# Four expert blocks instead of two at the tile-by-tile end of layer 0, three modulation steps moved there, hyena transposes two projections later

## The chip, the cores and the metric

The kernel is one program on one core of a Trainium2 chip. The time is device microseconds of one execution. TensorE is called PE here (its weight loads PEld), VectorE DVE, ScalarE ACT, GpSimd POOL, and SyncE, whose queue issues most DMAs, SP.

## The reference

Two layers run over 256 latent and 256 context tokens of width 1024, all in float32. In layer 1 the context tokens only feed the latent ones, so only the latent half is carried on. Cut to what matters here:

```python
for l in range(DEPTH):                                   # 2 layers
    mod = (silu(c) @ w_ada[l] + b_ada[l])                # six rows of 1024: sh1 sc1 g1 sh2 sc2 g2; the same for c_ctx
    y, yc = mixer_sublayer(x * (1 + sc1) + sh1, ...)     # one projection to 2824 columns, four mixers, one back
    x = layer_norm(alpha * x + g1 * y)
    x = layer_norm(alpha * x + g2 * peer(x * (1 + sc2) + sh2))

def hyena(p, ...):
    p = dwconv(p, short_w) + short_b                     # three taps
    x0, x1, v = split(p, 3, -1)
    u = v * x1
    y = bidir_fftconv(u, k_fwd, k_bwd) + u * skip
    return y * x0

def peer(h, wq, sub_keys, u_tab, v_tab):                 # per token: 8 heads x 16 of 16384 single-neuron experts
    q = h @ wq; top 16 of 128 for each of two halves; top 16 of their sums; g = softmax
    act = gelu(h . u_tab[e]); return sum_e (g * act) * v_tab[e]
```

## The kernel before

**Planner.** The program is written in an order, and a planner then orders each engine's queue before the run: it simulates the engines, and a free engine takes the earliest-written instruction that is ready in that simulation; `low(3000)` puts an instruction far behind. On the chip each engine then works its queue strictly in that order. A tile pool with `bufs=n` is a ring: the next tile of a name waits until the tile n places before it has been read for the last time. `issue_after` holds an instruction behind a named one on the same queue.

**Split.** Most products are made of float32 numbers cut in two: ACT casts the high part (line 140), POOL or DVE subtracts for the low part (line 141), and `mm3` multiplies three times (lines 144 to 146).

**Projections** (`mixers`, line 372 on). 128 columns at a time, `projT` loads a weight tile (512 KB, `w_raw`, ring of 4 in layer 1), splits it, and multiplies it with hT, the modulated input. Eight split products of 512 tokens make one projection in layer 0 and for keys, values and scan inputs in layer 1; of 256 tokens for the others of layer 1. The order is: four for the convolution, six for hyena (loop over `i` in 4, 2, 5, 3, 0, 1), four for the scan (loop over 2, 0, 1, 3), the scan's time steps, two gates, and then keys, queries and values. The 31 taps of the convolution (line 368) are written as low-priority filling on DVE. Hyena's product `hv[4+m] = hv[4+m] * hv[2+m]` (line 389) has to be transposed on PE (line 404); the transposes of half m = 1 are written behind the first scan projection, those of m = 0 behind the second.

**Modulation steps** (`ada_steps`, line 253 on). Step c of layer l makes 512 of the 6144 columns: four transfers of 512 KB (`wa_raw`, line 261), sixteen products (`pm`, line 263), a copy on ACT (line 267), four small transposes (`pt`, line 281) and an addition on DVE (`modT`, line 282). The steps are one generator, worked off in order by whoever calls it. In layer 0's router one part is called behind each of the query projections, and behind the last of them `fill_to(1, (FL, 11)[l])` works off all that is left up to step FL of layer 1. The buffer ring for `wa_raw` is 3 there. Layer 1's first projections need steps 0 to 3 of layer 1, its output projection 4 and 5, its expert stage the rest.

**Router** (layer 0). Sixteen query projections, the top-16 searches, `pairs` on DVE; then the slots are transposed (`tr`, line 1208), turned into one-hot tiles (`o`, `Ah`, `Al`, `B_`, lines 1226 to 1242), multiplied into gate blocks (`G`, lines 1248 and 1249), and stored to DRAM (`Gd`). Up to 28 blocks of the first expert product, `u_stage` (`au`: activations of 128 experts for 384 tokens, 24 products each), are written between these. Two stand ahead of the slots' transposes, seven ahead of the gates.

**Expert loop** (line 1378 on). For each of 128 blocks of 128 experts: `weights(bl)` multiplies the activations with the gates and splits them (`wh`, `wl`, ring of 4), `values(bl)` loads 512 KB (`v_raw`, ring of 2) and splits them (`v_hi`, `v_lo`, ring of 2), and `accum` adds 36 products to six PSUM banks (`ov`): three tiles of 128 tokens, two halves of 512 columns. The fourth tile of layer 0 is gathered row by row instead (`gathered`), two rows per block. The last NE = 2 blocks are kept out of the loop: for them each half tile in turn gets its products of both blocks, so that tile 0 is complete first. Behind each tile come `combine` (gate, residual, statistics, norm) and `to_hT` (transposes `xT`, line 792, scale, split into hT), from which layer 1's projections start. The value split of block 127 has a pool of its own (`vep`); its `v_raw` is of the ring. `fill_to(1, FX)` with FX = 6 stands in the last tile and finds nothing to do, since FL is 6.

Of the kernel before, what the change touches and what calls it, by code (L numbers as in the profile page):

```python
# [41 lines left out]
XB = (96, 100, 104, 108)  # L42
VD = (10, 1)
UM = ((0, 2, 4, 6, 7), (0, 1, 2, 3, 4, 5, 6, 7))
NE = 2
WHB = (4, 5)
WB = 3
PW = (1, 1)
PU = (0, 1)
PRB = (4, 5)  # L50
FL = 6
FM = 11
LF = 200
NF = 2
# [32 lines left out]
def tile_hybrid_diffusion(ctx: ExitStack, tc: tile.TileContext, I: dict, out: bass.AP):  # L87
    nc = tc.nc
    V, S, G, T = nc.vector, nc.scalar, nc.gpsimd, nc.tensor
    uid = [0]  # L90

    def pool(name, bufs=1, stack=ctx, **k):
        uid[0] += 1
        if "space" not in k:
            k["reuse_waits"] = "tile"
        return stack.enter_context(tc.tile_pool(name=f"{name}{uid[0]}", bufs=bufs, **k))
# [222 lines left out]
    def mixers(l, mx, wp, hT, yT, dfts, side, side_s, more):  # L319
# [70 lines left out]
        for i in (2, 0, 1, 3):  # L390
            n = NT if i == 3 else 512
            b = projT(18 + i, n)
            xc = t2k([128, 512])
            short_conv(xc[:, :n], b, "scw", "scb", i, n)
            sig(xb[:, i, :n], xc[:, :n])
            V.tensor_tensor(xb[:, i, :n], xb[:, i, :n], xc[:, :n], ALU.mult)
            next(side, None)
            with low(3000):
                next(taps, None)
            if i in (2, 0):  # L400
                m = i // 2
                b = bank("ut")
                for t in range(NTL):
                    T.transpose(b[:, t * 128:(t + 1) * 128], hv[:, 4 + m, t * 128:(t + 1) * 128], ident)
                S.copy(un[:, :, :, m * 128:(m + 1) * 128].rearrange("p t s c -> p s t c"), b[:, :NT].rearrange("p (s t c) -> p s t c", t=2, c=128))
# [407 lines left out]
    prep = {}  # L813
# [33 lines left out]
    for l in range(2):  # L847
# [426 lines left out]
        with ExitStack() as vst:  # L1274
# [17 lines left out]
            def values(bl, p, n, eng=G):  # L1292
                raw = mk(vp, [128, D], tag="v_raw", bufs=VB[l])
                late["v", bl] = nc.sync.dma_start(raw, I["v"][l, bl])
                hi = mk(p, [128, D], F32R, tag="v_hi", bufs=n)
                lo = mk(p, [128, D], F32R, tag="v_lo", bufs=n)
                split(raw, hi, lo, eng)
                return hi, lo
# [75 lines left out]
                nc.gpsimd.dma_start(xd[t], x_)  # L1374

            gat = gathered() if GT else iter(())
            last = 128 - NE
            for st in range(UBl, last + UBl):
                if st < 128:
                    u_stage(st)  # L1380
# [11 lines left out]
            ws, vs_ = [], []  # L1392
            for bl in range(last, 128):
                ws.append(weights(bl))
                if bl < 127 or l:
                    vs_.append(values(bl, vp, VB[l], V))
            rg_s.close()
            xp_s = ExitStack()
            x_n = mk(pool("xp", stack=xp_s, side="right"), [128, len(DT), D], name="x_n")
            fle = ExitStack()  # L1400
            if l == 0:
                vs_.append(values(127, pool("vep", stack=fle, side="right"), 1, V))
            end = tc.issue_after(late["v", 127 - VD[l]].ins)
            end.__enter__()
            for i, t in enumerate(DT):
# [20 lines left out]
            end.__exit__(None, None, None)  # L1426
            if l == 0:
                prep.clear()
                prep.update(raw=(pool("fl", stack=fle, side="right"), 3))
            for i, t in enumerate(DT):  # L1430
                for hh in range(2):
                    with tc.issue_after(prev.ins):
                        for j in range(NE):
                            ins = accum(last + j, i, *ws[j], *vs_[j], (hh,))
                    prev = ins
                if i == len(DT) - 1 - FI and l == 0:
                    fill_to(1, FX)
                lst = mk(gp, [128, 1, 2, 6], tag="ln_st")
                r = x_n[:, i, :]
                combine(t, r, gb[t // 2], lambda hh: pacc[i, hh], lst, lnr if l else None)  # L1440
                if l == 0:
                    to_hT([t], lambda t: x_n[:, DT.index(t), :], lnc, hT, gp, hb=HB2)
# [119 lines left out]
```

## Time and profile before

| | |
|---|---|
| median of 3 runs (lowest to highest) | 2898.36 us (2893.72 to 2905.68) |
| the profiled execution | 2899.02 us, span 2897.2 us, mean granted clock 0.967 |
| PE busy | 2688.0 us (93% of the span) |
| DVE busy | 1996.6 us (69%) |
| ACT, POOL busy | 1098.8 us (38%), 595.0 us (21%) |
| DMA | 625.03 MB, mean 216 GB/s |

The busy time is a mean over stages, so it has to be read stage by stage. On the time axis of the profiled execution layer 0's router ends at 605 us, its gates and first expert products run to about 790 us, its expert loop to 1784 us, the layers meet between 1784 and 1810 us, and layer 1's projections follow until about 1922 us. A matmul is pipelined, so two successive ones overlap in the rows.

### The profile page before, as it was taken

The numbers are of one execution on the slowest core, as the hardware profiler recorded it, in microseconds if no ns is written. First come the engines' busy times: TensorE is split into PE (matmuls) and PEld (weight loads), VectorE is DVE, ScalarE is ACT, GpSimd is POOL, SyncE is SP. The second block draws the span as 40 slices with busy tenths as digits, with TensorE's granted clock in tenths as the row PEclk, the third lists the DMA queues.
The fourth block names the chain that finished last, engine by engine and source line by source line (L and its number), as shares of the span: only waits on it lengthen the run. The fifth ranks groups of instructions, "written<-read, shape, count | busy, mean of one in ns | idle before, by whom it ended". The sixth has DMA issues, their size and how long they took to land.

```text
span 2897.2 us, 41097 instructions
## 1 busy us (share of the span) xinstructions
PE 2688.0 (93%) x15342; PEld 2283.5 (79%) x15342; DVE 1996.6 (69%) x4247; ACT 1098.8 (38%) x1736; POOL 595.0 (21%) x439
## 2 busy tenths in 40 slices
PE   6797899889899999999999998889999999999997
PEld 3574566578899988888878886766889899999986
DVE  4956448969787777777777746974866655555556
ACT  2233532235433333333323334334334444444443
POOL 2233000033224444444334202430000000000000
PEclk9899999989999999999999998899999999999999
DMA  7222433347899998999889735325458976776656
GB/s 258 59 91 95 131 131 113 131 143 270 284 325 309 314 333 309 317 308 317 305 299 308 250 103 195 99 99 186 131 157 295 309 235 204 216 216 202 196 189 196
DMA packets 241836, 625.03 MB, mean 216 GB/s; under 512 B 22424, under 2 KB 104794, under 8 KB 236004
## 3 DMA queue, kind: packets, MB, share of 16 engines
q1 hardware_dynamic: 201156, 475.05, 50.4%
q0 software_dynamic: 40480, 147.36, 14.3%
q8 instruction: 120, 1.97, 0.3%
q14 instruction: 80, 0.66, 0.1%
HBM read 573.04 MB, written 49.30 MB: 215 GB/s over the span
## 4 chain that ended last, share of the span: by engine, by line
PE 39%; DMA 13%; issue 11%; DVE 9%; POOL 6%; ACT 1%; SPq 0%; POOLq 0%; DVEq 0%; ACTq 0%
DMA grow<-in_vg_dram,eu 9%; PE ov L144 5%; PE ov L145 5%; POOL grow L1344 5%; PE ov L146 5%; PE au L1017 4%; PE au L144 4%; PE au L146 4%; PE au L145 4%; DMA grow<-in_lnr_dram 2%; DVE accg L1357 1%; DVE yT L368 1%; PE G L1248 1%; PE G L1249 1%; DMA grow<-in_ug_dram,eu 1%
## 5 line engine op out<-in xcount | busy, mean ns | idle before, releaser
L146 PE MATMUL au<-hT,u_lo 128*128 128x384 f32 (+1 forms) x1744 | 552.6, 317 | 5.6 <-DVE u_lo L141 5.2
L144 PE MATMUL au<-hT,u_hi 128*128 128x384 f32 (+1 forms) x1744 | 553.4, 317 | 3.0 <-DVE slT L1212 3.0
L145 PE MATMUL au<-hT,u_hi 128*128 128x384 f32 (+1 forms) x1744 | 551.6, 316 | 0.0
L145 PE MATMUL ov<-v_lo,wh 128*128 128x512 f32 x1280 | 505.0, 395 | 27.7 <-DVE v_lo L141 27.7
L146 PE MATMUL ov<-v_hi,wl 128*128 128x512 f32 x1280 | 500.8, 391 | 0.0
L144 PE MATMUL ov<-v_hi,wh 128*128 128x512 f32 x1280 | 462.9, 394 | 12.1 <-ACT v_hi L140 6.5
L140 ACT CAST u_hi<-u_raw 128x1024 fp32r<-128x1024 f32 x218 | 228.9, 1050 | 447.0 <-PE au L145 303.7
L141 DVE TENSOR_TENSOR v_lo<-v_raw,v_hi 128x1024 fp32r<-128x1024 f32 x255 | 312.6, 1227 | 78.9 <-ACT v_hi L140 78.3
L141 DVE TENSOR_TENSOR u_lo<-u_raw,u_hi 128x1024 fp32r<-128x1024 f32 x194 | 237.1, 1222 | 165.5 <-ACT u_hi L140 165.5
L144 PEld LDWEIGHTS au<-hT,u_hi 128*128 128x128 f32 x1744 | 332.1, 190 | 11.0 <-DVE slT L1212 3.4
L146 PEld LDWEIGHTS au<-hT,u_lo 128*128 128x128 f32 x1744 | 331.6, 190 | 9.6 <-DVE u_lo L141 8.3
L145 PEld LDWEIGHTS au<-hT,u_hi 128*128 128x128 f32 x1744 | 331.9, 190 | 7.7
L140 ACT CAST v_hi<-v_raw 128x1024 fp32r<-128x1024 f32 x256 | 268.1, 1047 | 107.2 <-DMA v_raw<-in_v_dram 98.6
L145 PEld LDWEIGHTS ov<-v_lo,wh 128*128 128x128 f32 x1280 | 242.1, 189 | 82.4 <-DVE v_lo L141 38.3
L140 ACT CAST wh<-act 128x384 fp32r<-128x384 f32 (+1 forms) x256 | 117.0, 459 | 464.5 <-PE ov L145 458.7
L144 PEld LDWEIGHTS ov<-v_hi,wh 128*128 128x128 f32 x1280 | 243.0, 190 | 57.4 <-ACT v_hi L140 6.7
L146 PEld LDWEIGHTS ov<-v_hi,wl 128*128 128x128 f32 x1280 | 241.8, 189 | 50.0
L1344 POOL DMA_INDIRECT grow<-in_vg_dram,eu x128 | 179.8, 1405 | 219.2 <-DVE accg L1357 167.8
L1357 DVE SCALAR_TENSOR_TENSOR accg<-grow,ag,accg 128x1024 f32<-128x1024 f32 x127 | 162.9, 1283 | 86.5 <-DMA grow<-in_vg_dram,eu 85.8
L1344 POOL DMA_INDIRECT grow<-in_ug_dram,eu x128 | 161.7, 1263 | 269.3 <-DVE grow L1348 234.0
L1348 DVE SCALAR_TENSOR_TENSOR grow<-grow,h2n 128x1024 f32<-128x1024 f32 x128 | 156.0, 1222 | 59.8 <-DMA grow<-in_ug_dram,eu 59.7
L141 DVE TENSOR_TENSOR wl<-act,wh 128x384 fp32r<-128x384 f32 (+1 forms) x256 | 125.3, 491 | 101.8 <-ACT wh L140 100.5
(834 smaller groups left out, 4194.1 us busy)
## 6 DMA issues: line engine op xcount, KB each, us to landing
u_raw<-in_uT_dram SPq DMA_DIRECT2D x256, 512.0 KB
v_raw<-in_v_dram SPq DMA_DIRECT2D x256, 512.0 KB
Gd<-stg SPq DMA_DIRECT2D x40, 1024.0 KB
gt<-Gd SPq DMA_DIRECT2D x80, 512.0 KB
wa_raw<-in_w_ada_dram SPq DMA_DIRECT2D x76, 512.0 KB
w_raw<-in_w_in_t_dram SPq DMA_DIRECT2D x44, 512.0 KB
w_raw<-in_wq_dram SPq DMA_DIRECT2D x32, 512.0 KB
w_raw<-in_w_ada_dram SPq DMA_DIRECT2D x20, 512.0 KB
```

The source lines that it names most:

```text
L140: S.copy(hi, src)
L141: late["V" if eng in (None, V) else "G"] = (eng or V).tensor_tensor(lo, src, hi.bitcast(F32), ALU.subtract)
L144: T.matmul(o, lh, rh, start=first, stop=False)
L145: T.matmul(o, lh, rl, start=False, stop=False)
L146: return T.matmul(o, ll, rh, start=False, stop=last)
L368: V.scalar_tensor_tensor(uc, upad[:, m, :, j:j + 256], wj, uc, op0=ALU.mult, op1=ALU.add)
L1017: T.matmul(b[:, :ND], raw[:, k, :], h32[0][:, k, :ND], start=k == 0, stop=k == 7)
L1248: T.matmul(b[:, j * 128:(j + 1) * 128], B_[:, tt // TC, :, tt % TC], Ah[:, tt // TC, :, tt % TC], start=True, stop=False)
L1249: T.matmul(b[:, j * 128:(j + 1) * 128], B_[:, tt // TC, :, tt % TC], Al[:, tt // TC, :, tt % TC], start=False, stop=True)
L1344: nc.gpsimd.indirect_dma_start(out=r, out_offset=None, in_=I[tab], in_offset=bass.IndirectOffsetOnAxis(ap=eu[:, i:i + 1], axis=0))
L1348: V.scalar_tensor_tensor(r, r, 1.0, h2n, op0=ALU.mult, op1=ALU.mult, accum_out=ag[:, i:i + 1])
L1357: V.scalar_tensor_tensor(accg, r, ag[:, i:i + 1], accg, op0=ALU.mult, op1=ALU.add)
```

## The change

Four things are changed. `NE` becomes a pair: 4 blocks are left for the tile-by-tile end of layer 0, 2 as before in layer 1. The value splits of blocks 126 and 127 get the separate pool, now of two buffers; those of 124 and 125 use the ring. `FL` becomes 3, so steps 4, 5 and 6 of layer 1's modulation are left over by layer 0's router and are worked off by `fill_to(1, FX)` behind the products of the last tile; the ring for their transfers there has 2 buffers instead of 3. In both layers hyena's transposes are written behind the third (half 0) and the fourth (half 1) scan projection.

```diff
-NE = 2
+NE = (4, 2)
...
-FL = 6
+FL = 3
...
-            if i in (2, 0):
+            if i in (1, 3):
                 m = i // 2
                 b = bank("ut")
...
-            last = 128 - NE
+            last = 128 - NE[l]
...
                 ws.append(weights(bl))
-                if bl < 127 or l:
+                if bl < 126 or l:
                     vs_.append(values(bl, vp, VB[l], V))
...
             if l == 0:
-                vs_.append(values(127, pool("vep", stack=fle, side="right"), 1, V))
+                vep = pool("vep", stack=fle, side="right")
+                for bl in (126, 127):
+                    vs_.append(values(bl, vep, 2, V))
...
-                prep.update(raw=(pool("fl", stack=fle, side="right"), 3))
+                prep.update(raw=(pool("fl", stack=fle, side="right"), 2))
...
                     with tc.issue_after(prev.ins):
-                        for j in range(NE):
+                        for j in range(NE[l]):
                             ins = accum(last + j, i, *ws[j], *vs_[j], (hh,))
```

## Rows read from the trace of the kernel before

**Rows 1.** Windows: busy PE, PEld, DVE, ACT, POOL (instructions), PE clock, DMA share, GB/s

```profile
605.00:763.00 158.00, 145.15 (x1288) 140.37 (x1288) 134.23 (x97) 80.77 (x143) 62.45 (x22) 0.97 0.63 219
...
790.00:1650.00 860.00, 827.86 (x4085) 744.19 (x4086) 663.45 (x1036) 288.11 (x395) 346.28 (x268) 0.99 0.91 312
...
1650.00:1775.00 125.00, 125.00 (x578) 106.39 (x577) 58.24 (x82) 45.64 (x65) 3.50 (x4) 1.00 0.41 127
...
1792.00:1810.00 18.00, 6.36 (x28) 5.18 (x27) 12.23 (x24) 12.04 (x19) 13.05 (x15) 0.59 0.44 136
...
1845.00:1859.00 14.00, 0.52 (x4) 0.28 (x3) 14.00 (x33) 1.72 (x2) 2.34 (x1) 0.67 0.24 85
```

**Rows 2.** Timeline, PE, layer 0's router: start us, us, line, output<-input, xcount, [idle before <-releaser]

```profile
579.44 2.92 PE L263 MATMUL pm<-wa_raw,s 128*32 128x256 f32 x24
...
603.31 2.08 PE L281 MATMUL pt<-sel,rw 128*128 128x128 f32 x8 [1.07 <-ACT rw L267]
...
605.04 0.67 PE L144 MATMUL au<-hT,u_hi 128*128 128x384 f32 x1
...
614.65 0.60 PE L1208 MATMUL tr<-cm,sl 128*128 128x128 f32 x4
```

**Rows 3.** Waits of DVE, 560 to 800 us: us in total, times, longest

```profile
DVE modT L282 <- PE pt L281: 3.1, 2, 2.6
...
DVE o L1226 <- ACT slT L1210: 8.0, 1, 8.0
...
DVE Ah L1239 <- PE G L1248: 15.2, 6, 9.1
```

**Rows 4.** Timeline of DVE behind the router

```profile
607.55 0.23 DVE L1163 COPY sl<-gw 128x128 f32<-128x128 f32 x1
...
624.34 4.56 DVE L1228 TENSOR_TENSOR o<-o,slT 128x2048 f16<-128x2048 f16 x2
...
720.57 1.21 DVE L1228 TENSOR_TENSOR o<-o,slT 128x2048 f16<-128x2048 f16 x1
```

**Rows 5.** Timeline of POOL there

```profile
620.46 2.87 POOL L141 TENSOR_TENSOR u_lo<-u_raw,u_hi 128x1024 fp32r<-128x1024 f32 x1 [2.21 <-ACT u_hi L140]
...
624.62 3.20 POOL L141 TENSOR_TENSOR u_lo<-u_raw,u_hi 128x1024 fp32r<-128x1024 f32 x1 [1.28 <-ACT u_hi L140]
```

**Rows 6.** Timeline of PE between the layers

```profile
1775.69 1.52 PE L144 MATMUL ov<-v_hi,wh 128*128 128x512 f32 x6
...
1783.85 0.39 PE L144 MATMUL ov<-v_hi,wh 128*128 128x512 f32 x1
...
1795.17 1.96 PE L792 MATMUL xT<-cm,x_n 128*128 128x128 f32 x8 [2.78 <-ACT x_n L1333]
...
1809.57 0.99 PE L144 MATMUL pj<-hT,w_hi 128*128 128x256 f32 x3
```

**Rows 7.** Timeline of SP between the layers

```profile
1762.23 16.52 SPq L1294 DMA_DIRECT2D v_raw<-in_v_dram  x5
```

**Rows 8.** Timeline of ACT between the layers

```profile
1782.30 1.05 ACT L140 CAST v_hi<-v_raw 128x1024 fp32r<-128x1024 f32 x1 [1.27 <-DMA v_raw<-in_v_dram]
```

**Rows 9.** Timeline of DVE between the layers and in layer 1

```profile
1783.38 1.23 DVE L141 TENSOR_TENSOR v_lo<-v_raw,v_hi 128x1024 fp32r<-128x1024 f32 x1 [1.10 <-ACT v_hi L140]
...
1809.44 0.69 DVE L141 TENSOR_TENSOR hT<-h,hT 128x512 fp32r<-128x512 f32 x1
...
1820.90 11.25 DVE L368 SCALAR_TENSOR_TENSOR yT<-upad,sm,yT 128x256 f32<-128x256 f32 x6
...
1883.96 1.23 DVE L141 TENSOR_TENSOR w_lo<-w_raw,w_hi 128x1024 fp32r<-128x1024 f32 x1
```

**Rows 10.** Timeline of PE at the hyena transposes, and at one later projection

```profile
143.61 0.66 PE L404 MATMUL ut<-cm,hv 128*128 128x128 f32 x4
...
1858.75 0.66 PE L404 MATMUL ut<-cm,hv 128*128 128x128 f32 x2 [13.48 <-DVE hv L389]
...
1887.76 0.40 PE L144 MATMUL pj<-hT,w_hi 128*128 128x512 f32 x1
```

## The prediction

> **What bounds the kernel now.** I read the busy time by stage first [rows 1]. In the expert loop PE is busy 828 of 860 us, and from 1650 to 1775 us all of 125: there the kernel is PE's, and what starts the loop later or earlier moves the end by as much. The change touches three stretches where PE is not the bound. At the end of layer 0's router (579 to 605 us) PE works off modulation steps behind their transfers. Between the layers (1792 to 1810 us) it has 6.4 us of work in 18. In layer 1's projections (1845 to 1859 us) it stands still and VectorE (DVE) is busy for the whole 14 us. The profiled execution took 2899.02 us, its span 2897.2; the median of the three runs is 2898.36, so the sum is made against 2899.0. About 0.5% (14.5 us) is what a measurement of this kernel can tell from no change.
>
> **Three modulation steps leave the router.** The timeline of PE shows the last three of the five steps that run in one block there: the first begins at 579.44 us, and the first expert block's u product follows at 605.04 us [rows 2]. They take 25.6 us, 8.5 each. Up to 25.6 us of PE can therefore come forward. But what PE does next feeds DVE. The list of DVE's waits from 560 to 800 us [rows 3] has 3.1 us for modT (the steps themselves, gone with them), 8.0 us for slT and 15.2 us for G, 9.1 of them in one piece. The slT wait is an order on PE: the last slot value was written at 607.8 us [rows 4], while the transpose of the slots stands on PE behind two u blocks and ran at 614.65 us [rows 2]. With PE 25 us ahead, its two u blocks are long done; transpose, copy and issue still need some 2 us, so 6 of 8 go. The 9.1 us wait is DVE waiting for the first gates' product behind seven more u blocks. PE can run some of these before the slots are ready: its two first blocks would end at 579.4 + 2 × 4.2 = 588, the slots without the modT waits and additions at about 604, and a u block takes 4.2 us (two successive splits start 4.16 us apart [rows 5]), so three to four fit; afterwards a G can still stand behind one block of 4.2 us, so I take 7 of 9.1 at most. Sum on DVE's side: 3.1 + 6 + 7 = 16 us. After that DVE paces the stage (134 us busy of 158 [rows 1]) and the loop behind it starts that much earlier; the store and reload of Gd between them keeps its length.
>
> Both bounds of this term: 25.6 us if PE's whole lead arrives; 7 us if the u blocks that move forward take it back. They bring POOL's u_lo splits, 2.4 to 3.2 us each [rows 5], under DVE's last routing steps. Rows 4 show the price: two L1228 products took 4.56 us together beside a split, one alone 1.21, thus 2.2 us for each split. Four of them cost 4 × 2.2 = 8.8 us, 16 − 8.8 = 7. I take 16, because those splits stand under DVE's work today too (at 616 to 640 us) and only change place.
>
> The Trainium skill, "SBUF — State Buffer", section Who interferes with whom, says the lock hits DVE instructions with two SBUF inputs or in a two-port mode, and no others. By that the search instructions of the routing tail would pay nothing and the term would stay nearer 16 than 7; the trace has no split beside a search instruction.
>
> **They arrive between the layers, behind a wait.** PE's accumulation of block 124 starts at 1775.69 us and the tile-by-tile end at 1783.85 [rows 6]: 8.16 us for two blocks, so a block costs 0.68 us per half tile. With four blocks left, the tile end starts at 1775.69, and the first half tile needs all of 124 to 127 at once. But v_raw has two buffers, and the change leaves that. SP issues one v_raw per 4.1 us, the last of the row at 1778.4 [rows 7]; v_hi of block 127 waited for that transfer and began at 1782.30 [rows 8]; v_lo followed at 1783.38 to 1784.6 [rows 9]. The issue of 127 waits for v_lo of 125, which waits for block 123 to leave the v_hi ring; none of that moves. So the first half tile still ends at about 1785.2, just as now, having done four blocks instead of the last two, while the rest of 124 and 125 (8.16 − 1.36 = 6.8 us) comes after it. PE's accumulation ends at about 1799 instead of 1792.4. Tile 1 ends at 1793.3 instead of 1789.4.
>
> What it buys is distance: the tiles come 5.5 us apart instead of 2.7, so their norms no longer pile up. Today PE gets the first transposes at 1795.17, 8.5 us after tile 0, and the first projection starts at 1809.57 [rows 6], 20.2 us after tile 1, when the lower part of hT (1809.44) arrives [rows 9]. Without the pile: 8.5 us to the transposes, 2 for them and 4 to 9.7 for scaling and splitting, 14.6 to 20.2 us after 1793.3, that is 1807.9 to 1813.5.
>
> Into this the three steps bring 12 transfers of 512 KB on SP's queue, 48 matmuls, 3 ACT copies, 12 small transposes and 3 additions. SP's order now is v_raw, x_n, then layer 1's w_raw; the steps' transfers go between, and because they have two buffers, not three, each of their later issues waits for PE's pm of two transfers before. Behind it stand the w_raw issues, and the first projections wait for these. One round is 3.8 us of transfer (1778.4 to 1782.25 [rows 7, 8]) plus 1.0 us for one buffer's pm (24 instructions, three buffers, in 2.92 us [rows 2]): 4.8 us for two transfers. Six pairs: the first lies ready, five rounds make 24 us, first products and tail another 4.7. If nothing runs before 1799, the last step ends at 1828. The 7 us in which PE waits for v are cover for about two pairs; then four remain: 1799 + 3 × 4.8 + 4.7 = 1818, with transposes and projections in the gaps. If that cover is missing, it costs the two rounds. I set the first projection at 1816.5, 7 us later than today; bounds 1807.9 (2 us earlier) and 1828 (19 us later).
>
> **Hyena transposes.** In layer 1 the pair for channel half 1 waits 13.5 us at 1858.75 for the last gating product [rows 10]. Two projections later that product is there: two 512-column projections take 2 × 24 × 0.227 = 10.9 us (0.227 is 8.16 us over 36 products [rows 6]), then channel half 0, then a half-size projection. PE would be 13.5 us ahead. But DVE is the bound: it is busy through the whole wait [rows 1], six convolution taps took 11.25 us beside POOL's splits, and w_lo of the next k projection, a DVE step behind all this, begins at 1883.96 [rows 9]. It ends at 1885.2, and that projection began at 1887.76 [rows 10], so at least 2.6 us are PE's own. More comes only if the planner puts some of the low-priority taps behind that split. I take 4, bounds 0 and 13.5. In layer 0 the same transposes wait for nothing (143.61, no idle time ahead [rows 10]); the move is worth 0 there, and ±1 from the order.
>
> The value ring, weights and act tiles do the same work in the same number; the row adds nothing: 0. Leaving four gather steps more behind the loop is covered, as the loop's last 125 us are PE's alone [rows 1].
>
> **Sum:** −16 + 7 − 4 = −13 us, 2899.0 − 13 = 2886.
>
> **Rivals.** *A, the likeliest:* as summed; each term off by some of its bounds gives 2873 to 2898. Chance 0.55.
>
> *B, the idle time fills:* the router gives 22, the steps fit wholly into the gaps between the layers (−2) and the taps make way (−11): −35, 2864. For it: 11.6 us without PE work between 1792 and 1810 [rows 1], and the 6.8 us for v. Against: two buffers and DVE's load. Chance 0.20.
>
> *C, the steps stand in front of layer 1, ending slower:* the planner puts all three ahead of the first projection, no pair runs under the wait for v, and w_raw waits on SP behind the twelfth transfer. Then 1828 + 3 us (cast and split of the first weights) is 21 us late, the hyena term is 0 because DVE's chain starts later with it. With 16 from the router: 2904; with 7: 2913. It decides once the first projection starts more than 16 us late, counted from the loop's end. Chance 0.15.
>
> *D, nothing gained at the router:* DVE's tail pays for the splits (−7) and the seam +7: 2899, no change. For it: behind its 9.1 us wait DVE has only 6.1 us of waits for G left [rows 3]. Chance 0.10.
>
> **How the numbers follow.** Predicted 2886. Faster by over 0.5% (below 2884): nearly half of A and all of B, 0.45. Slower by over 0.5% (above 2913): only the far half of C and what I do not see in the planner's order, 0.08. Within: 0.47. The range takes B's value at one end and C's nearer one at the other: 2864 to 2906.
>
> **What would show it.** Right: the first u product about 25 us earlier, DVE's slT wait near 2 and the G wait under 5; the loop starting 14 to 18 us earlier; PE idle 5 to 7 us at the start of the tile end, on v_hi or v_lo; pm rows among the transposes; the ut wait gone while DVE stays full until about 1880 (on today's clock). Wrong: no wait at the tile end (then the seam gains), the first projection over 16 us late, or PE starting k's projection over 8 us earlier relative to the first projection (then DVE was not the bound).

## The result: slower, and the profile of the changed kernel

The changed kernel takes 2930.22 us (median of 4 runs, 2923.34 to 2936.85), the kernel before 2896.04 us beside it (4 runs, 2893.66 to 2905.68): ratio 1.010, interval 1.0078 to 1.0123, thus 23 to 36 us slower. 2886 was predicted, with a range up to 2906. The profiled execution is the fastest of the four (2923.34 us, span 2921.6, mean granted clock 0.958); against that of before it is 24.3 us later at the end.

Five points of time, and the end, split these 24.3 us. The first three are the first u product, the loop's start (first product of activations and gates), and P, the last cast of `wh` in layer 0. P waits until block 123 has left the ring of four, so it lies where four blocks remain, whatever NE is. The last two are the first and the last projection of layer 1.

| us | before | after | difference |
|---|---|---|---|
| first u product | 605.04 | 582.00 | -23.0 |
| loop's start | 782.76 | 782.72 | 0.0 |
| P | 1775.67 | 1765.10 | -10.6 |
| P to the first projection | 33.9 | 68.5 | +34.6 |
| first to last projection of layer 1 | 110.9 | 111.5 | +0.6 |
| last projection to the end | 976.7 | 976.5 | -0.2 |

The seam costs 34.6 us where +7 was predicted. The timeline of PE there (columns as in [rows 2], and compare [rows 6]):

```profile
1774.08 0.79 PE L144 MATMUL ov<-v_hi,wh 128*128 128x512 f32 x1 [3.03 <-ACT v_hi L140]
...
1794.42 1.07 PE L263 MATMUL pm<-wa_raw,s 128*32 128x256 f32 x16
1798.61 1.08 PE L263 MATMUL pm<-wa_raw,s 128*32 128x256 f32 x8 [3.11 <-DMA wa_raw<-in_w_ada_dram]
...
1808.85 2.27 PE L263 MATMUL pm<-wa_raw,s 128*32 128x256 f32 x16 [3.57 <-DMA wa_raw<-in_w_ada_dram]
1815.75 1.08 PE L263 MATMUL pm<-wa_raw,s 128*32 128x256 f32 x8 [4.62 <-DMA wa_raw<-in_w_ada_dram]
...
1828.35 1.08 PE L263 MATMUL pm<-wa_raw,s 128*32 128x256 f32 x8 [1.60 <-DMA wa_raw<-in_w_ada_dram]
...
1833.62 0.56 PE L144 MATMUL pj<-hT,w_hi 128*128 128x256 f32 x1
```

The tile end begins at 1765.1, not at 1775.7, and stands still for v, as predicted, 3.03 us of it in the first row; its accumulation then ends at 1792.0. Between tile 1's transposes and the last tile's stand all three steps, from 1794.42 to 1832 us, with a wait for a transfer ahead of most groups of products. In before the first projection (1809.57 in [rows 6]) comes 1.6 us behind the last transposes, which stand at 1807.95; so it does here, at 1833.62. Why the transfers come so slowly, the timeline of SP shows, which answers to [rows 7]:

```profile
1764.15 2.42 SPq L261 DMA_DIRECT2D wa_raw<-in_w_ada_dram  x2
1767.85 0.33 SPq L1294 DMA_DIRECT2D v_raw<-in_v_dram  x1
...
1795.12 0.80 SPq L261 DMA_DIRECT2D wa_raw<-in_w_ada_dram  x2
1800.38 3.69 SPq L246 DMA_DIRECT2D w_raw<-in_w_in_t_dram  x2
1804.16 0.86 SPq L261 DMA_DIRECT2D wa_raw<-in_w_ada_dram  x2
...
1809.98 13.95 SPq L261 DMA_DIRECT2D wa_raw<-in_w_ada_dram  x6
```

Two transfers are issued at 1764, even ahead of the last v_raw, and the third not before 1795. The waits of SP from 1760 to 1835 us (us in total, times, longest):

```profile
SPq L261 <- PE pm L263: 28.4, 7, 22.1
SPq L246 <- POOL w_lo L141: 8.7, 3, 4.4
```

The 22.1 us are that third transfer's: it waits for the first step's products, and these stand in PE's queue behind the transposes of tile 1. From there each pair waits for products of the pair before, and in between SP stands in layer 1's w_raw issues, which wait 8.7 us for POOL's w_lo. The waits of PE in the same stretch:

```profile
PE pm L263 <- DMA wa_raw<-in_w_ada_dram: 16.9, 8, 4.6
PE ov L144 <- ACT v_hi L140: 3.9, 3, 3.0
...
PE ov L145 <- DVE v_lo L141: 2.0, 3, 0.8
```

From the first products (1794.42) to the twelfth transfer's (1828.35) five rounds take 33.9 us, 6.8 each; the prediction had 4.8. They are uneven. From a pair's first product to the next pair's it is 4.2, 10.2, 6.9, 5.1 and 4.9 us, and 2.7 to the twelfth transfer's; layer 1's w_raw issues stand ahead of the pairs that end the second and third of these, and of no other. In the last three a transfer's products come 3.7 to 5.8 us behind its issue, where 3.8 were reckoned, and its products take 1.08 us. The windows show the engines meanwhile, and DVE and PE at the hyena transposes (columns as in [rows 1]):

```profile
1765.00:1792.00 27.00, 21.16 (x73) 15.01 (x72) 13.31 (x21) 4.79 (x5) 5.18 (x8) 0.81 0.57 212
1792.00:1832.00 40.00, 20.07 (x138) 9.65 (x137) 10.91 (x18) 13.31 (x22) 11.08 (x9) 0.57 0.59 198
1882.00:1892.00 10.00, 1.01 (x9) 0.77 (x7) 9.96 (x25) 0.48 (x1) 0.00 (x0) 0.72 0.00 0
```

Against 6.4 us of work in 18 in [rows 1], PE has 20 us of work in 40 from 1792 to 1832, and a granted clock of 0.57, part of the time at 1.2 GHz: eight pm products take 1.08 us there (at 1815.75, granted clock 0.50) and 0.64 where the clock is full, as at 592.88 in before (granted clock 1.00):

```profile
592.88 0.64 PE L263 MATMUL pm<-wa_raw,s 128*32 128x256 f32 x8 [2.18 <-DMA wa_raw<-in_w_ada_dram]
```

Behind the wait for v too the clock falls (0.81 from 1765 to 1792); this is most of what takes the accumulation from the predicted 23.3 us behind P to 26.9.

At the router the first u product is 23.0 us earlier, and yet the loop starts at the same time. The waits of DVE from 560 to 800 us, which answer to [rows 3]:

```profile
DVE Ah L1239 <- PE G L1248: 23.2, 8, 12.8
...
DVE o L1226 <- ACT slT L1210: 4.7, 1, 4.7
```

The slots' wait for slT shrank from 8.0 to 4.7, the first wait for G, 9.1 in [rows 3], to 2.6 (at 640 us), and modT's are gone; but the waits for G are more than before, one of them 12.8 us. It comes behind two splits on POOL, in this timeline (compare [rows 5]):

```profile
697.25 3.14 POOL L141 TENSOR_TENSOR u_lo<-u_raw,u_hi 128x1024 fp32r<-128x1024 f32 x1 [5.86 <-ACT u_hi L140]
707.26 18.84 POOL L141 TENSOR_TENSOR u_lo<-u_raw,u_hi 128x1024 fp32r<-128x1024 f32 x2 [6.87 <-ACT u_hi L140]
```

and beside this stretch of DVE's timeline:

```profile
701.59 1.21 DVE L1239 TENSOR_TENSOR Ah<-o,o 128x2048 f16<-128x2048 f16 x1
...
720.36 1.21 DVE L1242 TENSOR_TENSOR B__1001_5794<-iE,slT 128x2048 f16<-128x2048 f16 x1
734.39 1.23 DVE L1239 TENSOR_TENSOR Ah<-o,o 128x2048 f16<-128x2048 f16 x1 [12.82 <-PE G L1248]
```

The split that begins at 697.25 begins at 703.81 in before: up to here the gates are 6.6 us ahead, and no more. Then two splits take 18.84 us together, where two like those of [rows 5] take 6. From 701.59 to 721.6 DVE runs without a gap products that read two operands in SBUF; the second split ends at 726.1, PE's u block and the gates' product stand behind it, and DVE waits 12.82 us at 734.39. The first of the two lasts 16.51 us, to 723.77, 2.2 us beyond the end of DVE's row; a split with nothing beside it takes 2.4. The profile of before has no such pair (its 22 splits in the gates take 2.84 us in the mean).

Ahead of the gates the slots are no earlier than before: the last one is written at 609.96 us, in before at 607.55 [rows 4]; about 604 was predicted. The search before them stands 2.9 us later in this execution (its last cast, line 1108, at 584.52 against 581.59), and one DVE instruction of the tail now runs beside a POOL split that came forward (595.40 to 597.83). It is first shown in before, then in after:

```profile
592.48 0.22 DVE L1156 TENSOR_SCALAR tf<-tf 128x128 f32<-128x128 f32 x1
```

```profile
595.55 2.37 DVE L1156 TENSOR_SCALAR tf<-tf 128x128 f32<-128x128 f32 x1
```

P is 10.6 us earlier although the loop started at the same time, so these 10.6 us are not the router's: the loop itself was shorter. From its 8th to its 120th block the queues of PE, ACT and SP hold the same instructions in the same order in both kernels; what differs is how long PE waits for the splits. Its waits for them from 783 to 1765 us (us in total, times, longest), in before and then in after:

```profile
PE ov L145 <- DVE v_lo L141: 26.8, 23, 5.4
...
PE au L146 <- DVE u_lo L141: 5.2, 8, 1.5
```

```profile
PE ov L145 <- DVE v_lo L141: 22.6, 16, 5.2
...
PE au L146 <- DVE u_lo L141: 1.5, 3, 0.7
```

From the loop's start to P it is 992.9 us in before and 982.4 in after, and between 978 and 994 in the 17 profiles of this document.

### The profile page after: what moved, and what is told of

The parts are those of the page before. It is cut to its first block, busy times and chain, and to the rows that moved or that the text cites. A ratio compares the mean times of both kernels' runs of the same rounds, so it can differ in the third digit from the quotient of the medians.

```text
span 2921.6 us, 41098 instructions
## 1 busy us (share of the span) xinstructions
PE 2695.7 (92%) x15342; PEld 2291.3 (78%) x15342; DVE 1994.9 (68%) x4247; ACT 1101.8 (38%) x1738; POOL 603.2 (21%) x439
## 3 DMA queue, kind: packets, MB, share of 16 engines
q8 instruction: 120, 1.97, 0.3%
## 4 chain that ended last, share of the span: by engine, by line
PE 41%; DMA 12%; issue 11%; DVE 9%; POOL 6%; ACT 1%; SPq 0%; POOLq 0%; DVEq 0%; ACTq 0%
DMA grow<-in_vg_dram,eu 7%; PE ov L145 5%; PE ov L144 5%; PE ov L146 5%; POOL grow L1344 5%; PE au L1017 5%; PE au L144 4%; PE au L146 4%; PE au L145 4%; DVE yT L368 1%; DVE accg L1357 1%; DMA grow<-in_lnr_dram 1%; PE G L1248 1%; PE G L1249 1%; DMA wa_raw<-in_w_ada_dram 1%
## 5 line engine op out<-in xcount | busy, mean ns | idle before, releaser
L1344 POOL DMA_INDIRECT grow<-in_vg_dram,eu x128 | 173.8, 1358 | 217.1 <-DVE accg L1357 171.1
```

Source lines behind the costliest of these rows:

```text
L1344: nc.gpsimd.indirect_dma_start(out=r, out_offset=None, in_=I[tab], in_offset=bass.IndirectOffsetOnAxis(ap=eu[:, i:i + 1], axis=0))
```

## Experiments

All ratios are to the kernel before, measured beside each kernel; "P" and "seam" (P to the first projection) are from the profiled execution of each kernel. The medians carry the comparison; a run of before itself lies between 2887 and 2917 us. A profile is one execution: P holds what the loop's own waits add, and the seam differs by 4.6 us between two kernels whose program is the same there (one_step_and_hyena and one_step_hyena_dve_splits, 38.0 and 42.6).

| kernel | median, us | ratio, interval | P | seam |
|---|---|---|---|---|
| before | 2900 | 1 | 1775.7 | 33.9 |
| after | 2930.2 | 1.010 [1.0078, 1.0123] | 1765.1 | 68.5 |
| steps_alone | 2919.8 | 1.0072 [1.0045, 1.0099] | 1764.3 | 59.9 |
| blocks_alone | 2909.3 | 1.0027 [1.0000, 1.0054] | 1775.0 | 38.1 |
| hyena_alone | 2901.7 | 0.9998 [0.9972, 1.0024] | 1786.2 | 33.9 |
| change_without_seam_steps | 2926.2 | 1.0087 [1.0065, 1.0109] | 1765.0 | 38.9 |
| router_term_alone | 2895.1 | 0.9979 [0.9958, 1.0000] | 1773.5 | 34.0 |
| seam_one_transfer | 2898.4 | 0.9995 [0.9968, 1.0022] | 1761.6 | 41.8 |
| steps_from_first_tile | 2915.1 | 1.0048 [1.0025, 1.0071] | 1772.3 | 55.5 |
| steps_from_first_tile_two_blocks | 2906.9 | 1.0026 [1.0004, 1.0047] | 1767.0 | 50.1 |
| steps_five_buffers | 2909.1 | 1.0032 [1.0017, 1.0047] | 1764.9 | 53.7 |
| one_step_and_hyena | 2891.3 | 0.9978 [0.9962, 0.9994] | 1760.9 | 38.0 |
| two_steps_first_tile_hyena | 2897.4 | 0.9980 [0.9961, 0.9999] | 1770.5 | 38.5 |
| gate_splits_on_dve | 2880.6 | 0.9920 [0.9894, 0.9945] | 1759.7 | 34.0 |
| router_term_dve_splits | 2867.0 | 0.9885 [0.9847, 0.9924] | 1738.9 | 34.0 |
| change_dve_splits | 2906.7 | 1.0016 [0.9996, 1.0037] | 1742.2 | 68.0 |
| one_step_hyena_dve_splits | 2871.8 | 0.9901 [0.9867, 0.9935] | 1743.7 | 42.6 |

### The parts one by one

Each is the kernel before with one part of the change: the steps (ring of 3 kept), the four blocks with `vep` of two, or the transposes.

```diff
-FL = 6
+FL = 3
```

> The kernel before with one edit, the three modulation steps moved from the router to the seam (three raw buffers as before, two expert blocks in the tile end, hyena transposes as before). Theory 1 (the loss of the whole change is that the steps stand on PE between the transposes of the second and of the last tile, and layer 1's projections behind them): 15 to 28 us slower than before, first projection 20 to 30 us late counted from the loop's end, nothing gained at the router. Rival (the loss comes from the four blocks and the two buffers for v; the steps alone bring what the prediction said, 16 us at the router for a few at the seam): 5 to 16 us faster.

19 us slower, seam 59.9 us, 26 later: theory 1 holds for the seam. Its "nothing gained at the router" this profile doesn't decide: the loop starts at 782.76, as in before, behind a pair of splits of 18.84 us, and the 11 us by which P is earlier arise in the loop.

```diff
-NE = 2
+NE = (4, 2)
```

> The kernel before with one edit, four expert blocks of layer 0 in the tile end with a ring of two for the last two; all six steps stay at the router, hyena transposes as before. Theory 1: PE waits some 6 us for v at the start of the tile end as in the changed kernel, but the tiles end further apart, so the first projection starts within 5 us of before: -3 to +5 us. Rival (the wait for v and the lower clock behind it carry the loss): 10 to 20 us slower.

The seam is 4.2 us longer, inside the expectation; the ratio (0 to 16 us slower) allows a little more. The wait for v and the lower clock are not the greater part of the loss.

```diff
-            if i in (2, 0):
+            if i in (1, 3):
```

> The kernel before with one edit, the hyena transposes two projections later in both layers. Theory 1 (DVE bounds that stretch): 0 to 6 us faster, PE's wait of 13.5 us for the gating product gone, DVE full until about 1880 as before, PE waiting elsewhere. Rival (PE bounds it): 9 to 14 us faster.

No difference that the runs show (-8 to +7 us). In the profile the stretch from the first to the last projection is 107.9 us, 3.0 shorter; but over all profiles it is 110.1 in the mean where the transposes are moved (9, from 107.8 to 113.4) and 111.0 where they aren't (8, from 109.8 to 113.2). The edit moves half 0 by one projection and half 1 by three. PE's new wait, behind the transposes that now wait for nothing, with what stands ahead of it on DVE and ACT:

```profile
1866.36 0.38 PE L404 MATMUL ut<-cm,hv 128*128 128x128 f32 x2
...
1877.86 0.73 DVE L345 SCALAR_TENSOR_TENSOR t2k<-pj,sm,t2k 128x510 f32<-128x510 f32 x1
...
1878.68 0.63 ACT L149 ACTIVATE xb<-t2k 128x512 f32<-128x512 f32 x1 [21.00 <-issue]
1879.21 0.23 ACT L140 CAST w_hi<-w_raw 128x64 fp32r<-128x64 f32 x1
...
1879.49 0.60 PE L144 MATMUL pdt<-hT,w_hi 128*8 128x512 f32 x1 [9.66 <-ACT w_hi L140]
```

The 13.5 us of [rows 10] became 9.7 at the product for the scan's time steps (`pdt`), which waits for the cast of its weights. That cast stands in ACT's queue behind an activation that reads what DVE finishes at 1878.6, and DVE runs without a gap up to there: PE still waits for DVE, by way of ACT's queue. The three parts add up, 19 + 8 + 0 = 27 us, against 23 to 36 for the whole.

Then the change with its steps taken from the seam:

```diff
-FX = 6
+FX = 3
```

> The changed kernel with the three steps not at the seam but among layer 1's mixers, where steps 7 to 11 are already made (steps 1, 2 and 3 at the router as in the change). Theory 1: 20 to 30 us faster than the changed kernel, that is 2892 to 2905, for the pm products and their waits between 1794 and 1832 us are gone. Rival (the four blocks carry the loss): stays above 2912.

A miss for theory 1's total: the seam shrinks to 38.9 us, but the kernel stays 25 us slower. The steps now stand among layer 1's mixers, ahead of the output projections, and the stretch from the last projection of the mixers to the first output projection grows from 78.8 to 111.4 us. PE waits there too for the steps' transfers, now in the ring of the weights:

```profile
2004.64 1.08 PE L263 MATMUL pm<-w_raw,s 128*32 128x256 f32 x8 [4.14 <-DMA w_raw<-in_w_ada_dram]
```

So it isn't the seam alone that is a bad place; three steps made where they are needed cost some 30 us in either. PE's waits for their transfers are 7.6 us in this stretch; what the rest is made of was not taken apart.

### What the steps cost at the seam

```diff
+                raw = prep.get("one")
+                if raw is None:
+                    raw = mk(pr, [128, 8, 128], ...)
+                    wdma[0] = nc.sync.dma_start(raw, I["w_ada"][l, 2 * c4 + j, q])
+                    if "one" in prep:
+                        prep["one"] = raw
...
-                prep.update(raw=(pool("fl", stack=fle, side="right"), 2))
+                prep.update(raw=(pool("fl", stack=fle, side="right"), 2), one=None)
...
+                    prep.pop("one")
```

> The changed kernel, with one transfer in place of the seam's twelve: all 48 products of the three steps read the one weight tile that was loaded first, so the modulation values are wrong; products, copies and transposes stay in number and place. Theory 2a (the twelve transfers through two buffers set the price of the steps at the seam): the 38 us from the first pm to the last transposes shrink to about 22, that is 13 products' groups of 1.08 us, three copies and three groups of transposes of 2.07 us; 12 to 18 us faster than the changed kernel. Rival 2b (the place alone, in front of the projections, sets it): under 6 us faster.

The seam falls from 68.5 to 41.8 us and the kernel to the time of before, more than theory 2a gave. Its timeline of PE has the products of the first two steps, the last transposes, and the first projection; the three steps stand where they stood in after:

```profile
1788.14 1.93 PE L267 MATMUL pm<-wa_raw,s 128*32 128x256 f32 x32
...
1793.89 3.28 PE L267 MATMUL pm<-wa_raw,s 128*32 128x256 f32 x32
...
1802.60 1.04 PE L796 MATMUL xT<-cm,x_n 128*128 128x128 f32 x8
...
1803.39 0.37 PE L144 MATMUL pj<-hT,w_hi 128*128 128x256 f32 x1
```

The first step's 32 recorded products take 1.93 us, one behind the other; in after they are one group of 1.07 and two of 1.08, with waits between. The seam's 34.6 us are therefore 4.2 for the four blocks, 3.7 for products, copies and transposes (41.8 against 38.1 with the blocks alone; a difference of one profile to another, no larger than the 4.6 us above), and 26.7 for the transfers: 16.9 of PE's own waits, and what comes with them, the lower clock among it (0.89 from 1760 to 1805 us here).

Opening the steps earlier, with four blocks and two buffers, or with two blocks and three:

```diff
-FI = 0
+FI = 2
```

> The changed kernel, with the three steps opened at the first tile of the end and not at the last (four blocks, two raw buffers): the first products stand on PE among the accumulation of tile 2. Theory 2a (twelve transfers in six rounds of 6.6 us set it): the rounds begin at about 1765 with the first buffers' loads and end near 1810, so the first projection comes 48 to 55 us after the point where four blocks remain, not 68.5: 13 to 20 us faster than the changed kernel. Rival (a product that waits for its transfer holds up the accumulation behind it, and the tiles' norms come late): no faster, or slower.

> The kernel before with the three steps at the seam, opened at the first tile of the end, three raw buffers, two blocks, hyena as before. Theory 2a: against the same steps opened at the last tile (19 us slower than before) 10 to 18 us better, that is 0 to 9 us slower than before. If the router's gain of some 14 us holds, the first projection stands 10 to 20 us later than before, counted from the point where four blocks remain. Rival (products on PE hold up the accumulation): 15 to 25 us slower than before.

Both do what theory 2a said, the first seam half a microsecond above what it gave: the seam falls to 55.5 and 50.1 us, 13 and 10 less than from the last tile, and the medians by 15 and 13. Products inside the accumulation cost less than the rounds that they start earlier. Then more buffers (the steps alone, ring of 5):

```diff
-                prep.update(raw=(pool("fl", stack=fle, side="right"), 3))
+                prep.update(raw=(pool("fl", stack=fle, side="right"), 5))
```

> The kernel before with the three steps at the seam as in the run with the steps alone, but five raw buffers for them, not three. Theory 3 (the price is the rounds of transfers that cannot be issued before a buffer comes free: 59.9 us from the point where four blocks remain to the first projection with three buffers, 41.8 in the changed kernel with one transfer in all): five of twelve transfers lie ready, the first projection comes at 48 to 56 us after that point, 8 to 15 us faster than with three buffers. Rival (transfer rate, not buffers): 57 us or more, no faster.

53.7 us and 2909: 6 us less seam and 11 us less time than with three. The size of the ring counts, then, and not the rate alone.

### Where the router's lead goes

First without the three steps anywhere:

```diff
-FL = 6
+FL = 3
...
+            if l == 1 and 4 <= c <= 6:
+                V.memset(modTs[1][:, MC[c]:MC[c] + 4, :], 0.0)
...
+                continue
```

> The kernel before, with the three modulation steps taken from the router and done nowhere: their 12 values per channel are set to zero at the seam, so layer 1's mixer gate and half of a shift are wrong. What is left is the router term alone. Theory 2 (the router keeps most of what the prediction said; at the point where four blocks remain the three kernels without the steps stand 14 us ahead of the three with them): 8 to 18 us faster than before, u product about 22 us earlier. Rival (the gates behind it take the lead back, as the loop's equal start in the first pair of profiles says): 0 to 4 us faster.

6 us faster (0 to 12), between the theories. Counted from the search's last cast (line 1108), the profiles tell how far the lead gets, as means of the three kernels with the steps at the router and POOL's splits (before, blocks_alone, hyena_alone) and of the eight without:

| us from the search's last cast | with | without | lead | predicted |
|---|---|---|---|---|
| last slot written | 25.5 | 25.2 | 0.3 | 3.1 |
| first one-hot tile (behind slT) | 34.8 | 30.6 | 4.2 | 9.1 |
| behind the first wait for G | 65.2 | 55.3 | 9.9 | 16 |
| loop's start | 204.5 | 195.9 | 8.6 | 16 |

Up to the wait for G no profile is more than 1.2 us from its mean. The instruction of line 1156, 0.22 us long in the three, takes 2.37 in all eight, beside a POOL split that came forward; this takes back most of the 3.1. The loop's start scatters by 8 and 13 us, and the profiles say why: a pair of splits that takes 10.2 or 18.8 us stands in 8 of the 11 experiments with splits on POOL, in two of them twice, with the steps at the router (blocks_alone, hyena_alone) and without. In hyena_alone, whose router is that of before, POOL's timeline has:

```profile
687.31 10.23 POOL L141 TENSOR_TENSOR u_lo<-u_raw,u_hi 128x1024 fp32r<-128x1024 f32 x2 [8.47 <-ACT u_hi L140]
...
722.02 18.89 POOL L141 TENSOR_TENSOR u_lo<-u_raw,u_hi 128x1024 fp32r<-128x1024 f32 x2 [6.83 <-ACT u_hi L140]
```

and in steps_from_first_tile:

```profile
662.48 18.85 POOL L141 TENSOR_TENSOR u_lo<-u_raw,u_hi 128x1024 fp32r<-128x1024 f32 x2 [6.87 <-ACT u_hi L140]
...
710.45 18.89 POOL L141 TENSOR_TENSOR u_lo<-u_raw,u_hi 128x1024 fp32r<-128x1024 f32 x2 [6.83 <-ACT u_hi L140]
```

Each pair of 18.8 us is followed by a wait of DVE for G of about 12 us, each of 10.2 by one of 7.4. The three kernels with the steps at the router have three such pairs, the eight without have seven, about one in each: they scatter the loop's start, but that they take the lead back is not shown. P scatters by 11 to 12 us among kernels with the same router; its mean is 1779.0 for the three with the steps there and 1766.7 for the eight without, 12 us apart, of which 10 stand at the loop's start already.

To test what POOL's splits do, those of the gates' u blocks go to DVE, in a stage where DVE was thought full:

```diff
-UEV = (0, 0)
+UEV = (1, 0)
...
-                            u_stage(bl, G, PU[l])
+                            u_stage(bl, V if UEV[l] else G, PU[l])
```

> The kernel before with the u_lo splits of the gates' stage on VectorE and not on GpSimd, nothing else. Theory 4 (the long splits, 10.2 and 18.8 us for a pair, come from VectorE's unbroken rows of products with two inputs, and they are what takes back part of the router's lead and spreads the runs): no split over 3 us and no wait of VectorE for G over 10 us in the profile; the splits cost VectorE 1.2 us each, 22 of them 27 us, less 1 to 2 us each that its products lose beside a GpSimd split: 5 us faster to 10 us slower, runs spread less. Rival (the long splits have another cause): waits for G of 7 us and more remain, 15 us slower or more.

23 us faster (16 to 31), better than either expected. The waits of DVE from 560 to 800 us:

```profile
DVE u_lo L141 <- ACT u_hi L140: 31.5, 13, 4.8
DVE act L1286 <- DMA gt<-Gd: 5.5, 2, 4.4
```

No wait for G is left. The window of the gates in [rows 1], here:

```profile
605.00:763.00 158.00, 151.83 (x1362) 147.54 (x1363) 128.03 (x126) 86.14 (x151) 1.12 (x1) 0.97 0.63 228
```

DVE is busy 128.0 us with 126 instructions, the splits among them, against 134.2 with 97 in [rows 1]: its products beside POOL's splits had cost more than the splits themselves do. One group of these products, from 605 to 763 us in before and then here (busy us, mean ns, idle time before):

```profile
L1239 DVE TENSOR_TENSOR Ah<-o,o 128x2048 f16<-128x2048 f16 x24 | 41.7, 1745 | 15.2 <-PE G L1248 15.2
```

```profile
L1239 DVE TENSOR_TENSOR Ah<-o,o 128x2048 f16<-128x2048 f16 x24 | 29.0, 1218 | 0.0
```

Whether the runs spread less isn't clear: 10 us in these four, 29 in the seven of one_step_hyena_dve_splits.

> The three steps done nowhere (12 values per channel zero, as in the run of the router term alone) and the gates' u_lo splits on VectorE. Open is why the router gave about 6 us and not 16. Theory 5 (GpSimd splits under VectorE's products took the rest back): without them the lead of 22 to 26 us on PE arrives as the 10 to 16 us of VectorE's former waits: 10 to 16 us faster than the run with the splits on VectorE (2881), that is 2865 to 2871. Rival (VectorE's own chain from the router's search to the first gates is the bound, whoever splits): 3 to 8 us, 2873 to 2878.

With the splits on DVE the router term is 2880.6 - 2867.0 = 13.6 us by the medians of four runs each, inside what theory 5 gave; by the two ratios it is 10, and their intervals overlap. The profiles don't bear theory 5 out: from the search's last cast the lead is 10.6 us behind the first wait for G, where it was 9.9 with POOL's splits, and 7.9 at the loop's start, where it was 8.6. That POOL's splits had taken back the rest of the 16 is not shown.

> The changed kernel with the gates' u_lo splits on VectorE. Theory 3 (the change's loss is the seam's, 34.6 us, and the gates only add the run's spread): the loss stays, 18 to 28 us slower than the kernel before with the same splits (2881), that is 2899 to 2909. Rival (a good part of the loss is the long splits that the change's order of u blocks brings about): under 12 us of loss, below 2893.

The change stays 26 us slower than the same splits without it (2906.7 against 2880.6), its seam 68.0 us: the loss is the seam's.

### Versions that beat both

Only the last of the steps goes to the seam, with five buffers, and hyena's transposes move; then with one more left over and opened at the first tile; then the former with the splits on DVE:

```diff
-FL = 6
+FL = 5
...
-            if i in (2, 0):
+            if i in (1, 3):
...
-                prep.update(raw=(pool("fl", stack=fle, side="right"), 3))
+                prep.update(raw=(pool("fl", stack=fle, side="right"), 5))
```

> A version that may beat both: the kernel before with only the last of the steps at the seam, whose four transfers all lie ready in five raw buffers, and the hyena transposes two projections later. Theory 3: no transfer to wait for, so the step costs its products, copy and transposes, some 4.8 us in a gap of 4 to 5: first projection at 34 to 37 us after the point where four blocks remain (33.9 before); router 2 to 4 us, hyena 3 us: 2 to 7 us faster. Rival (each step costs a third of what three cost): first projection at 42 us, 2 us slower.

> The kernel before with two of the three steps at the seam, opened at the first tile of the end, five raw buffers, and the hyena transposes two projections later. Theory 3: five of eight transfers lie ready, the other three are issued while the accumulation still runs; first projection at 37 to 44 us, router 4 to 7 us, hyena 3 us: between 6 us faster and 2 us slower than before. Rival (products on PE hold up the accumulation and the norms behind it): first projection at 45 us or later, 4 to 10 us slower.

> A version to beat both: one step at the seam with five raw buffers, hyena transposes later, and the gates' u_lo splits on VectorE. If the terms add: 2881 less 6, that is 2870 to 2880, and 20 to 30 us faster than before. If the router's part needs the GpSimd splits' place to show: 2880 to 2884.

6 us faster (2 to 11) with one step, whose four transfers lie ready: seam 38.0 us, one more than expected. 6 us (0 to 11) with two. With the DVE splits 0.990, 19 to 39 us faster than before, inside the first expectation; its seam of 42.6 us is 4.6 longer than without these splits, with the same instructions on PE: the granted clock in it is 0.74 against 0.85 (46 us from P on), and the first and the last group of transposes take 1.97 and 1.92 us there, 1.09 and 1.04 without.

## Why the prediction failed, point by point

**The seam's steps: the term that was mis-sized.** It decides the result: without the transfers the time comes out near that of before (2898.4 in seam_one_transfer). The whole seam was to grow by 7 us; the steps alone added 30.4 of the 34.6 (26.7 + 3.7). Three assumptions of that paragraph fell. First, "the 7 us in which PE waits for v are cover for about two pairs": the steps are written in the last tile, and the planner placed them behind tile 1's transposes; none ran under the wait, and a queue of PE is worked in order. That was rival C's placement, to which 0.15 was given, though `fill_to` being written in the last tile spoke for it. Second, a round of 4.8 us for two transfers: it took 6.8. SP's queue also carries the w_raw issues, which wait for POOL, and these were named as standing behind the steps but not between them; they stand in the long second round (10.2), but not in the last two, in which the transfers and the products at the lower clock took longer than reckoned. Third, the gap that was to hide products was reckoned as PE's idle time. It was wide enough for the products (3.7 us when the transfers are gone), but PE's waits for the ring of two came on top (the 26.7 us), and no work of PE stood there to hide them. Even rival C, with 1831 us (55 behind P), stayed 13 short of the 68.5 measured.

**The four blocks.** The wait for v was predicted as 5 to 7 us at the start of the tile end and is 5.9 (3.9 + 2.0 in PE's waits). The first projection without steps was put at 32.2 to 37.8 us behind P; blocks_alone has 38.1. Right in mechanism, just above its upper bound, and the lower granted clock behind the wait was not foreseen.

**The router.** 16 predicted; 6 (0 to 12) by the medians of router_term_alone, 8.6 by the profiles at the loop's start, 0.0 in the first pair of profiles. The first u product came forward as forecast (23 us, 25 said), and the first wait for G shrank to 2.6 us (under 5 said). The step that failed is the sum 3.1 + 6 + 7: behind the first gates it is 0.3 + 3.9 + 5.7 = 9.9 us. The 3.1 for modT were to bring the slots forward, to about 604 us; an instruction of the tail, held beside a split that came forward, took 2.1 of them back. The wait for slT kept 4.7 us, not 2. So the lower bound's mechanism acts at one place, ahead of the slots, where the prediction had the splits "only change place"; without POOL's splits the lead is hardly larger (10.6 us with them on DVE). In the first pair of profiles the lead was 6.6 us at 697 us, and a pair of long splits, which the execution of before has none of, took it. That P was 10.6 us earlier even so is luck: the loop, which the change leaves alone, waited less.

The Trainium skill's rule ("SBUF — State Buffer", section Who interferes with whom), as the prediction cites it, names both sides: instructions with two SBUF inputs or in a two-port mode, and no others. By it the searches pay nothing, and so they do: the search's FIND_INDEX8 instructions beside splits take 0.29 us in before (528.9 to 529.7 us) and 0.20 in after (from 589.24 us), as long as those without one. The prediction's "the trace has no split beside a search instruction" was thus wrong. But the routing tail isn't searches alone, and the instruction that paid is a TENSOR_SCALAR.

**Hyena.** -4 predicted, -3 in the profile of hyena_alone, -1.0 in the mean over all profiles, nothing in the changed kernel (+0.6), as rival C said. The mechanism, DVE as the bound, was right: from 1882 to 1892 us in after DVE is busy 9.96 us of 10 while PE has 1.01. What was mis-sized is what PE could gain past it: the wait only moved, to the product whose weights ACT casts behind DVE's work.

**The sum.** By the profiled executions 37.3 us were missed (+24.3 instead of -13): 27.6 at the seam, 16 at the router and 4.6 at hyena, less 10.6 in the loop and 0.2 behind the projections, which no term of the sum stands for. The medians lie 34 apart, 10 more than the profiles: after's profiled execution was its fastest, 7 us under its median, and that of before lay 3 above the median beside it. The range's upper end of 2906 was said to be rival C's nearer value; that is 2904.

## What to carry to other kernels

Work that is moved into another engine's idle time brings its transfers along: count how many lie ready in the ring when the gap begins, and price the others one by one in rounds through that ring and through every issue that shares the queue; only the first kind is hidden. Look where a planner will put the moved work in the order of each queue before counting any wait as its cover. Read a lead at the end of the stage that made it: further on, another stage's waits are added to it. And where a split on GpSimd runs beside VectorE products with two SBUF operands, try it on VectorE even if VectorE looks full.

## What the runs showed of the hardware

A POOL split of 2.4 us that begins within an unbroken row of DVE products with two SBUF inputs can last beyond the end of that row: pairs of 10.2 and 18.8 us, in eleven places of thirteen profiles, and only these two lengths. In all eleven the first split of the pair (7.9 or 16.5 us) ends 2.2 us behind the end of DVE's row, wherever it began, as if it did its work only then. Most splits in such rows take 2.4 to 3.5 us, and a DVE product beside them 2.7 to 3.4 instead of 1.21. Which execution gets a long one was not controlled. The same section of the Trainium skill's page "SBUF — State Buffer", Who interferes with whom, says that the second of the two engines to issue is blocked until the first one's instruction is finished; here 16.5 us passed in one split beside products of 1.2 us each, so the block did not end with one instruction. That the row of products is what holds it is argued from the times, the 2.2 us of all eleven above all; that the splits on POOL cause the waits for G is shown by moving them. The same splits on DVE take 1.22 us each, and 87 instructions of the gates 95.6 us in gate_splits_on_dve, where they take 131.0 in before.

PE's granted clock in the seam of after was 0.57, and the same eight pm products took 1.08 us there and 0.64 at full clock: here, products that waited for transfers also ran slower.
